# A weighted sum of expert outputs: loads 4 to 10 issued from GpSimd's queue instead of SyncE's

## The chip, the cores and the metric

The kernel runs on one core of a Trainium2 chip. The metric is the device time of one execution, in microseconds (us). The profile comes from one execution recorded by the hardware profiler. DVE is VectorE, ACT is ScalarE, POOL is GpSimd, SP is SyncE and PE is TensorE. "SPq", "ACTq" and "POOLq" are the instruction streams of these engines where they issue transfers.

## The reference

For every token there are two rows of 512 float32 numbers (the outputs of its two experts) and two weights. The result is the weighted sum of the two rows.

```python
batch, seq, hidden, k = 16, 1024, 512, 2
expert_outputs   # (16, 1024, 2, 512) float32, 67.1 MB
combine_weights  # (16, 1024, 2) float32, 0.13 MB
out = np.sum(expert_outputs * combine_weights[..., None], axis=2)   # (16, 1024, 512), 33.6 MB
```

There are 16,384 tokens. For each, 4 KB are read and 2 KB are written, and three arithmetic operations are made for each output number.

## The kernel before

The tokens are dealt out over the 128 partitions of the on-chip memory, 128 to each. The work goes in eleven groups, numbered 0 to 10 by the loop variable `g`. Groups 0 to 9 hold 12 tokens in each partition (6,144 KB to load, 3,072 KB to store), group 10 holds 8 (4,096 KB and 2,048 KB).

Each group has one tile `et` from a pool with four buffers (L50, `bufs=4`). The result of a group is written over the first half of its own tile (`ot`, L66). So a group uses one buffer from its load to the end of its store, and load `g` cannot be issued before store `g-4` has landed. Loads 0 to 3 find free buffers at the start.

For groups 0 to 8, DVE multiplies the whole tile by the weights, which are repeated along 512 columns (L74), and adds the two halves (L75). I call these mult `g` and add `g`. ACT's queue then issues the store (L76). For group 9, ACT scales the first expert's rows (L82, 12 instructions) while DVE scales the second's (L97), and DVE adds them (L98). For group 10, ACT scales one token's row at a time (L82, 8 instructions) and DVE multiplies and adds (L86, 8 instructions). The stores of groups 9 and 10 are issued by SP (L99). The weights come by two small loads from ACT's queue (L58). They are computed on by nothing else.

Who issues what, before: SP issues all eleven loads (L69) and stores 9 and 10. ACT issues the weights and stores 0 to 8. POOL sets four constants at the start and then issues nothing. Each engine works through its own stream in program order, and an instruction that waits holds up all those behind it in that stream. A transfer issued by an engine goes into that engine's transfer queue. The profile calls SP's q1 and ACT's q10. The order of the instructions within each stream is chosen by the framework's scheduler when the kernel is built. It comes from the loop, but is not bound to it.

Before, DVE's stream is mult 0, add 0, mult 1, add 1 and so on to mult 8, add 8, and then L97, L98 and the eight L86. ACT's stream is the two weight loads, stores 0 to 7, eight of group 9's scalings, store 8, the other four scalings, and group 10's eight.

Of the kernel before, what the change touches and what calls it, by code (L numbers as in the profile page):

```python
# [1 line left out]

# [4 lines left out]


@with_exitstack
def kernel(  # L10
    ctx: ExitStack,
    tc: tile.TileContext,
    expert_outputs: bass.AP,
    combine_weights: bass.AP,
    out: bass.AP,
):

    nc = tc.nc  # L20
    b, s, k, h = expert_outputs.shape
    assert k == 2
    n = b * s
    P = nc.NUM_PARTITIONS
    per = n // P
    assert per * P == n
    J, LAST = 12, 8
    main = per - LAST
    assert main % J == 0
    eo = expert_outputs.rearrange("b s k h -> (b s) (k h)")  # L30
    cw = combine_weights.rearrange("b s k -> (b s) k")
    o = out.rearrange("b s h -> (b s) h")

    def rows(x):

        a = x[0 : P * main, :].rearrange("(p t) f -> p t f", p=P)
        b = x[P * main : n, :].rearrange("(p t) f -> p t f", p=P)
        return lambda t, c: a[:, t : t + c, :] if t < main else b[:, t - main : t - main + c, :]

    eo, cw, o = rows(eo), rows(cw), rows(o)  # L40

    dt = mybir.dt.float32
    mult = mybir.AluOpType.mult
    add = mybir.AluOpType.add
    copy = mybir.ActivationFunctionType.Copy

    last = main // J

    wpool = ctx.enter_context(tc.tile_pool(name="w", bufs=1))
    ipool = ctx.enter_context(tc.tile_pool(name="in", bufs=4))  # L50

    wt = wpool.tile([P, per * k], dt)

    warm = wpool.tile([P, 1], dt)
    table = nc.scalar.activation(out=warm, in_=nc.const_aps.tensor(1.0, (P, 1), dt), func=copy)  # L55
    with tc.issue_after(table.ins):
        for t, c in ((0, main), (main, LAST)):
            nc.scalar.dma_start(  # L58
                out=wt[:, k * t : k * (t + c)].rearrange("p (t k) -> p t k", k=k), in_=cw(t, c)
            )  # L60


    for g in range(last + 1):
        et = ipool.tile([P, J, k * h], dt)

        ot = et.rearrange("p j f -> p (j f)")[:, 0 : J * h].rearrange("p (j f) -> p j f", f=h)  # L66
        t0, c = g * J, J if g < last else LAST

        nc.sync.dma_start(out=et[:, 0:c], in_=eo(t0, c))  # L69
        if g < last - 1:  # L70

            wb = wt[:, g * J * k : (g + 1) * J * k].unsqueeze(2).to_broadcast([P, J * k, h])
            ek = et.rearrange("p j (k h) -> p (j k) h", k=k)
            nc.vector.tensor_tensor(out=ek, in0=ek, in1=wb, op=mult)  # L74
            nc.vector.tensor_tensor(out=ot, in0=et[:, :, 0:h], in1=et[:, :, h : 2 * h], op=add)  # L75
            nc.scalar.dma_start(out=o(t0, c), in_=ot)  # L76
            continue


        for i in range(c):  # L80
            t = t0 + i
            nc.scalar.activation(  # L82
                out=et[:, i, 0:h], in_=et[:, i, 0:h], func=copy, scale=wt[:, 2 * t : 2 * t + 1]
            )
            if g == last:
                nc.vector.scalar_tensor_tensor(  # L86
                    out=ot[:, i, :],
                    in0=et[:, i, h : 2 * h],
                    scalar=wt[:, 2 * t + 1 : 2 * t + 2],
                    in1=et[:, i, 0:h],  # L90
                    op0=mult,
                    op1=add,
                )
        if g < last:
            w1 = wt.rearrange("p (t k) -> p t k", k=k)[:, t0 : t0 + c, 1:2]
            x1 = et[:, :, h : 2 * h]
            nc.vector.tensor_tensor(out=x1, in0=x1, in1=w1.to_broadcast([P, c, h]), op=mult)  # L97
            nc.vector.tensor_tensor(out=ot, in0=et[:, :, 0:h], in1=x1, op=add)  # L98
        nc.sync.dma_start(out=o(t0, c), in_=ot[:, 0:c])  # L99


# [1 line left out]
_INS = ['expert_outputs', 'combine_weights']  # L103
_OUTS = [((16, 1024, 512), 'float32')]


# [23 lines left out]
```

## Time and profile before

| what | value |
|---|---|
| time, median of 3 runs | 239.14 us (239.09 to 239.26) |
| the profiled execution: own time | 239.1 us |
| its span in the trace | 237.3 us |
| DVE busy | 194.0 us (82%) |
| ACT busy | 14.0 us (6%) |
| POOL busy | 0.2 us |
| bytes moved | 100.80 MB |
| share of the 16 DMA engines: q1 (SP), q10 (ACT) | 71.0%, 27.9% |
| a mult (L74), an add (L75) | 12.96 us, 6.56 us |
| issue to landing, median: a load of SP, a store of ACT | 29.9 us, 33.0 us |

The profiled execution took 239.1 us, 0.04 below the median of the runs. Its span, from the first instruction to the last, is 237.3 us, so 1.8 us lie around the span. The share of a queue is the time that its packets took, as a share of the whole time of the 16 DMA engines, so the two shares say how nearly the transfers fill the span. "Issue to landing" contains the time that a transfer stands in its queue behind earlier ones, and the time in which it shares the DMA engines with the other queue.

### The profile page before, as it was taken

The numbers are of one execution on the slowest core, as the hardware profiler recorded it, in microseconds if no ns is written. First come the engines' busy times: TensorE is split into PE (matmuls) and PEld (weight loads), VectorE is DVE, ScalarE is ACT, GpSimd is POOL, SyncE is SP. The second block draws the span as 40 slices with busy tenths as digits, with TensorE's granted clock in tenths as the row PEclk, the third lists the DMA queues.
The fourth block names the chain that finished last, engine by engine and source line by source line (L and its number), as shares of the span: only waits on it lengthen the run. The fifth ranks groups of instructions, "written<-read, shape, count | busy, mean of one in ns | idle before, by whom it ended". The sixth has DMA issues, their size and how long they took to land.

```text
span 237.3 us, 153 instructions
## 1 busy us (share of the span) xinstructions
DVE 194.0 (82%) x28; ACT 14.0 (6%) x22; POOL 0.2 (0%) x4
## 2 busy tenths in 40 slices
DVE  0008999999999999999999879969996998785710
ACT  2000000000000000000000000000000000740800
POOL 0000000000000000000000000000000000000000
DMA  7999999989899999999897999999997979999997
GB/s 268 422 524 398 398 415 514 398 356 505 356 439 431 431 464 464 398 398 522 348 522 344 452 431 431 464 464 398 398 522 340 530 340 456 458 403 442 406 434 309
DMA packets 3456, 100.80 MB, mean 425 GB/s; under 512 B 512, under 2 KB 640, under 8 KB 640
## 3 DMA queue, kind: packets, MB, share of 16 engines
q1 hardware_dynamic: 1872, 72.35, 71.0%
q10 hardware_dynamic: 1584, 28.44, 27.9%
HBM read 67.24 MB, written 33.55 MB: 425 GB/s over the span
## 4 chain that ended last, share of the span: by engine, by line
DMA 59%; DVE 33%; ACT 2%; DVEq 0%; ACTq 0%; issue 0%; SPq 0%
DMA out_dram<-et 29%; DMA et<-in_expert_outputs_dram 23%; DVE et L74 22%; DVE et L75 11%; DMA wt<-in_combine_weights_dram 7%; ACT et L82 2%; DVE et L86 1%; DVEq L125 0%; ACTq L125 0%; ACT L55 0%; SPq L69 0%; DVEq L74 0%; ACTq L82 0%
## 5 line engine op out<-in xcount | busy, mean ns | idle before, releaser
L74 DVE TENSOR_TENSOR et<-et,wt 128x12288 f32<-128x12288 f32 x9 | 116.6, 12955 | 25.1 <-DMA wt<-in_combine_weights_dram 18.4
L75 DVE TENSOR_TENSOR et<-et 128x6144 f32<-128x6144 f32 x9 | 59.0, 6557 | 0.3
L82 ACT ACTIVATE et<-et,wt 128x512 f32<-128x512 f32 x20 | 12.5, 707 | 210.2 <-DMA et<-in_expert_outputs_dram 210.2
L86 DVE SCALAR_TENSOR_TENSOR et<-et,wt 128x512 f32<-128x512 f32 x8 | 5.6, 746 | 3.9 <-ACT et L82 3.7
L97 DVE TENSOR_TENSOR et<-et,wt 128x6144 f32<-128x6144 f32 x1 | 6.6, 6558 | 2.2 <-DMA et<-in_expert_outputs_dram 2.2
L98 DVE TENSOR_TENSOR et<-et 128x6144 f32<-128x6144 f32 x1 | 6.6, 6558 | 0.9 <-ACT et L82 0.9
L55 ACT ACT_TABLE_LOAD x1 | 1.3, 1283 | 0.7 <-PEq L114 0.7
L55 ACT ACTIVATE warm<-const-float32-1.0 128x1 f32<-128x1 f32 x1 | 0.2, 204 | 0.0
L114 POOL MEMSET const-bfloat16-1.0<- 128x1 bf16 x1 | 0.1, 103 | 0.0
L114 POOL MEMSET const-uint8-127<- 128x1 uint8 x1 | 0.1, 103 | 0.0
L114 POOL MEMSET const-float32-1.0<- 128x1 f32 x1 | 0.1, 100 | 0.0
L114 POOL MEMSET const-float32-0.0<- 128x1 f32 x1 | 0.1, 99 | 0.2 <-issue 0.2
## 6 DMA issues: line engine op xcount, KB each, us to landing
et<-in_expert_outputs_dram SPq DMA_DIRECT2D x10, 6144.0 KB, 29.9
out_dram<-et ACTq DMA_DIRECT2D x9, 3072.0 KB, 33.0
et<-in_expert_outputs_dram SPq DMA_DIRECT2D x1, 4096.0 KB, 25.1
out_dram<-et SPq DMA_DIRECT2D x1, 3072.0 KB, 14.7
out_dram<-et SPq DMA_DIRECT2D x1, 2048.0 KB, 10.0
wt<-in_combine_weights_dram ACTq DMA_DIRECT2D x1, 120.0 KB, 17.5
wt<-in_combine_weights_dram ACTq DMA_DIRECT2D x1, 8.0 KB, 31.8
```

Of the source, the lines that this page charges most:

```text
L55: table = nc.scalar.activation(out=warm, in_=nc.const_aps.tensor(1.0, (P, 1), dt), func=copy)
L74: nc.vector.tensor_tensor(out=ek, in0=ek, in1=wb, op=mult)
L75: nc.vector.tensor_tensor(out=ot, in0=et[:, :, 0:h], in1=et[:, :, h : 2 * h], op=add)
L82: nc.scalar.activation(out=et[:, i, 0:h], in_=et[:, i, 0:h], func=copy, scale=wt[:, 2 * t : 2 * t + 1])
L86: nc.vector.scalar_tensor_tensor(out=ot[:, i, :], in0=et[:, i, h : 2 * h], scalar=wt[:, 2 * t + 1 : 2 * t + 2], in1=et[:, i, 0:h], op0=mul ...
L97: nc.vector.tensor_tensor(out=x1, in0=x1, in1=w1.to_broadcast([P, c, h]), op=mult)
L98: nc.vector.tensor_tensor(out=ot, in0=et[:, :, 0:h], in1=x1, op=add)
L114: nc = _bacc.Bacc("TRN2", target_bir_lowering=False, num_devices=1)
```

## The change

Loads 0 to 3 are still issued by SP. Loads 4 to 10 are issued by POOL. Nothing else in the source is different but for an empty line that is gone, so all line numbers after it are smaller by one in the profile of the changed kernel.

```diff
-        nc.sync.dma_start(out=et[:, 0:c], in_=eo(t0, c))
+        (nc.sync if g < 4 else nc.gpsimd).dma_start(out=et[:, 0:c], in_=eo(t0, c))
```

What each load waits for is as before: load `g` (4 and up) waits for store `g-4`. The scheduler, however, puts DVE's and ACT's streams in another order when it builds the changed kernel:

```
DVE before: ... mult 3, add 3, mult 4, add 4, mult 5, add 5, mult 6, add 6, mult 7, add 7, mult 8, add 8, L97, L98, ...
DVE after:  ... mult 3, mult 4, add 3, add 4, mult 5, mult 6, add 5, add 6, mult 7, mult 8, add 7, add 8, L96, L97, ...
ACT before: stores 0 to 7, 8 scalings of group 9, store 8, 4 scalings of group 9, 8 of group 10
ACT after:  stores 0 to 6, 11 scalings of group 9, stores 7 and 8, 1 scaling of group 9, 8 of group 10
```

SP's stream after the change is loads 0 to 3, store 9, store 10. POOL's is its four constants and then loads 4 to 10.

## The prediction

> **What bounds the kernel now.** I read the page's totals first, then the slices, then the span cut into stretches, then the chain and the queue's waits, and last the issue times. The page:
>
> ```profile
> span 237.3 us, 153 instructions
> DVE 194.0 (82%) x28; ACT 14.0 (6%) x22; POOL 0.2 (0%) x4
> ...
> DVE  0008999999999999999999879969996998785710
> ...
> DMA  7999999989899999999897999999997979999997
> ...
> q1 hardware_dynamic: 1872, 72.35, 71.0%
> q10 hardware_dynamic: 1584, 28.44, 27.9%
> HBM read 67.24 MB, written 33.55 MB: 425 GB/s over the span
> ```
>
> DVE looks like the busiest engine, but it has holes in the first 18 us and in the last third. The row of DMA has none: the two queues take 98.9% of the DMA engines' span. The same by stretches of about one group (columns: stretch and length, busy time of DVE, ACT and POOL, clock, DMA share, GB/s):
>
> ```profile
> 18.40:38.00 19.60, 19.53 (x3) 0.00 (x0) 0.00 (x0) 1.00 1.02 442
> 38.00:57.40 19.40, 19.36 (x3) 0.00 (x0) 0.00 (x0) 1.00 0.97 405
> ...
> 96.30:115.80 19.50, 19.47 (x3) 0.00 (x0) 0.00 (x0) 1.00 0.99 429
> ...
> 135.40:157.20 21.80, 19.50 (x2) 0.00 (x0) 0.00 (x0) 1.00 1.00 433
> 157.20:181.00 23.80, 19.53 (x3) 0.00 (x0) 0.00 (x0) 1.00 0.99 430
> 181.00:203.00 22.00, 19.60 (x3) 0.09 (x1) 0.00 (x0) 1.00 1.00 430
> ```
>
> The DMA share is 0.97 or more in every stretch from 0.73 us to 220. From 135 us on, DVE has 2 us to spare in every group. It waits for bytes. The chain that ended last and the longest wait of SP's queue say how the bytes are ordered:
>
> ```profile
> 76.94 30.65 DMA out_dram<-et
> 107.59 0.02 SPq L69
> 107.61 0.03 issue
> 107.64 29.93 DMA et<-in_expert_outputs_dram
> ...
> SPq L69 <- DMA out_dram<-et: 189.4, 7, 61.2
> ```
>
> Store 2 lands and load 6 is issued into its buffer, so SP's 189.4 us of waiting are waits for buffers. That wait is not lost time: while load 6 waits to be issued, load 5 is still in SP's queue. The times of issue show the pace:
>
> ```profile
> 64.14 0.33 SPq L69 DMA_DIRECT2D et<-in_expert_outputs_dram  x1
> ...
> 85.93 0.33 SPq L69 DMA_DIRECT2D et<-in_expert_outputs_dram  x1
> ...
> 107.64 0.33 SPq L69 DMA_DIRECT2D et<-in_expert_outputs_dram  x1
> ...
> 226.48 0.34 SPq L99 DMA_DIRECT2D out_dram<-et  x1
> ```
>
> Loads follow one another at 21.75 us, and in that time one load and one store move: 9.437 MB in 21.75 us is 434 GB/s. So the kernel is bound by the DMA engines, which finish whatever stands in the queues. From that rate a load costs 14.5 us of all DMA engines, a store 7.25, load 10 9.67, store 10 4.83 and the weights 0.3. All of it: 10 x 14.5 + 9.67 + 10 x 7.25 + 4.83 + 0.3 = 232.3 us. The last store was issued at 226.48 and took 10.0 to land (the page's issues), so it landed at 236.5. That leaves 4.2 us for the start and all losses on the way. The question about any new order is therefore only: **is there a moment at which all queues are empty?** Each microsecond of such a hole is a microsecond of the result, and nothing else is.
>
> **The change, part by part.**
>
> *Seven issues leave SP, seven come to POOL.* An issue costs SP 0.33 us x 7 = 2.3 us, beside 189.4 us of waiting, so nothing comes free. On SP, stores 9 and 10 stood behind the loads, but went out when L98 and L86 were done, not when SP was free. Their gain is 0. POOL has nothing else after its constants (0.2 us), so nothing is queued behind the new waits there but the next loads, in the order that they had on SP.
>
> *The delay T from the end of a load's wait to its first byte.* No row shows POOL issuing. Lower end: SP's own. The first slice of 5.93 us moved 268 GB/s x 5.93 = 1.59 MB, which is 3.7 us at 434, so bytes flowed from about 2.2 us. The first issue was at 0.73, so T is 1.5 us there. Upper end: POOL is held until the running DVE instruction ends, at most a mult, T = 1.5 + 12.96 = 14.5 us. I take 2.5, near the lower end, because an issue on another engine is the nearest row. What T costs depends on how long the queues last without that load, which I work out below.
>
> *A third queue.* Load 4 is issued at about 64 us, while SP's queue still holds some of load 3. Before, it stood behind load 3, which landed at 72.3 in the trace. Now three queues share. A transfer has 144 packets (1872 of q1 by its 13), 9 for each of 16 DMA engines, and the 128 partitions make 8 of them data: a piece is an eighth, 14.5/8 = 1.81 us for a load and 0.91 for a store. From 64.1 to 72.3 there is room for three pieces of each, so three eighths of load 3 remain, and each now also lets an eighth of load 4 pass: load 3 lands up to 3 x 1.82 = 5.5 later, at 77.7. Mult 3 began at 76.83, so at most 0.9 us of DVE are lost, and load 4 is earlier by as much as load 3 is later. The same bytes move, so cost on the DMA engines is 0. SP's queue is empty after that, and there are two again, POOL's in the place of SP's.
>
> *DVE's new order.* Mult 4 now goes before add 3, so store 3 leaves late. Mult 3 ends at 89.8. Load 4, which landed at 94.0 before (64.14 + 29.9), lands at 92 to 94. Mult 4 then ends at 105 to 107 and add 3 at 111.6 to 113.6. Before, store 3 was issued at 96.40. It is 15 to 17 us late, and load 7 behind it. Meanwhile the queues hold loads 0 to 5 and stores 0 to 2: 6 x 14.5 + 3 x 7.25 + 0.3 = 109.1 us of work, finished between 2.2 + 109.1 = 111.3 and 4.2 + 109.1 = 113.3. What must arrive before that is load 6. Its wait ends when store 2 lands, 107.6 before and up to 1.8 later now (store 1 and 2 also share with load 4). With T = 2.5 it flows at 110.1 to 111.9. So **the first thin place is at about 112 us**, with 0 to 3 us in hand. What is lost there is at most the time until store 3 takes over, about 1.1 us. I take 0.2, as the two intervals hardly overlap.
>
> *The other thin places.* Store 3 and load 6 end at about 134, and load 7 is issued then. Store 4 (add 4 ended 6.6 after add 3, at 118 to 120) waits in ACT's queue and fills 7.25 us: in hand 7.25 - T. Store 4 lands at 147 and releases load 8 with 5 eighths of load 7 to go (9 us in hand). Mult 5 and 6 fill 119 to 145, add 5 ends at 152 and store 5 follows. Store 5 and load 8 end at 178, when store 6 (issued at 158) is in the queue alone: again 7.25 - T for load 9. Store 6 lands at 190, load 10 follows, and load 9 lasts until 200. Load 10 moves alone from 200 to 209.
>
> *ACT's new order.* Store 7 now stands behind eleven scalings that wait for load 9. Add 7 ends at about 197, load 9 lands at 200, and eleven scalings took 6.8 us before, so store 7 leaves by 207 at the latest, and flows at 208.5: before load 10's 9.67 us are over. Cost 0, but with only 1 us in hand. If ACT's queue runs ahead of its scalings (before, store 8 was issued at 203.01, 0.1 us after the first of the eight scalings ahead of it began), there are several. Stores 7 and 8 then fill the time to 224, store 9 (L97 of the changed kernel ends at about 217) to 231, and store 10 (the eight L85 end at 223) to 236. Cost 0. DVE's whole lateness of some 4 us at the last groups lies behind 7 us of queued stores.
>
> *The rate of a load in POOL's queue.* Lower end 0 (same bytes, same pieces). Upper end: the slowest stretch of a group, 38.0 to 57.4, moved 405 GB/s, 7% below 434, and that on 6 x 14.5 + 9.67 = 96.7 us is 6.8 us. I take 0.2, near the lower end, since the stretches at 429 to 442 are the rule.
>
> A rule of the Trainium skill speaks against the change. "SBUF — State Buffer", section "SBUF: two separate sides", says that transfers issued from GpSimd have their descriptors written by GpSimd's cores, and that a DVE instruction in a two-port mode shuts these out until it ends. A mult here takes 12.96 us for 12,288 elements, 1.05 ns each, and has two SBUF inputs. For such instructions the page limits the blocking to GpSimd work that reads SBUF. By that page, writing descriptors would go on, and the sum would stay. If the blocking held, the sum would be that of the first rival. No row of this case shows which.
>
> **Sum.** 237.3 + 0.2 (thin place at 112) + 0.2 (rate) = 237.7 of span, and 1.8 around it: 239.5 us. The profiled execution's 239.1 stands 0.04 below the median, so this is no change by the bound of 0.2% (0.48 us), about what a measurement of this kernel can tell.
>
> **The rivals.**
>
> 1. *POOL is held by DVE (slower).* DVE is busy nearly without a gap from 38 to 200, and each held issue waits for the end of a mult or add. The place that decides is load 7: wait over at 134, when mult 6 has just begun, so issued at 147 and flowing at 148.5 to 149. Store 4 ends at 141. The hole is 7 to 8 us, and a second one of up to 3 can open near 207, at load 10. It decides from a hold of about 5 us on. For it: POOL has not issued anything here beside DVE, so nothing speaks against it in the rows. Against it: POOL's four settings of constants took 0.10 us each, but with DVE idle, so this says little. 237.3 + 7 to 11: 246 to 250 us, and 243 to 246 if only half of a hold is met.
> 2. *The turns are dealt out otherwise.* The pieces of SP and ACT alternate. If POOL's come in larger bundles, a store waits behind most of a load, load 6 is released late and holes of some 2 us open at 112, 158 and 202, up to 5 in all: 241 to 244. If they come in thirds or smaller, stores pass faster, load 4 lands later (98), DVE ends 7 us later and stores 7 and 8 run out before store 9: a hole of 2, 241.
> 3. *Loads from POOL's queue run slower.* Each per cent is 1 us. 1 to 3%: 240.1 to 242.
> 4. *Faster.* It could only come from the 4.2 us that aren't bytes, of which 1.5 + 0.7 are the start. Of the 2.0 left, perhaps 0.5 to 1 goes when loads and stores overlap differently: 238.3 to 238.6. Nothing in the rows points to it.
>
> That the change does nothing is excluded by the streams: POOL has seven loads.
>
> **How the numbers follow.** No hole worth naming: 0.42, with its own range 239.0 to 239.6, and 239.5 in it. Rival 1: 0.16. Rival 2: 0.16. Rival 3: 0.20. Rival 4: 0.06. So faster 0.06, same 0.42, slower 0.52: the cases of slower together outweigh the likeliest single one. Below 239.0 I leave 0.08. Above 244.5 lies some two thirds of rival 1, 0.11. The range is 239.0 to 244.5.
>
> **What would show it.** Right: DMA shares of 0.97 and more in all stretches, loads 7 and 9 flowing before their covering store has ended, SP's wait of 189.4 us gone from its queue and standing in POOL's, store 3 issued at 112 to 114, DVE's last instruction a few us before the last store. Wrong: a stretch at 110 to 113, 134 to 149 or 200 to 210 with a DMA share well under 1 (rivals 1 and 2), or full shares at fewer GB/s (rival 3). The prediction falls if T is above 5 us.

## The result and the profile after

| | before | changed |
|---|---|---|
| median time (5 runs of each, taken in turns) | 239.09 us (238.94 to 239.26) | 241.39 us (241.20 to 242.05) |
| ratio, with its 95% interval | | 1.0094 (1.0071 to 1.0117) |
| the profiled execution: time, span | 239.10, 237.32 us | 241.51, 239.74 us |

The changed kernel is slower by 0.94%, or 2.3 us. The time around the span is the same (1.78 and 1.77 us), so all the difference lies inside the span. The page of the changed kernel:

```profile
span 239.7 us, 156 instructions
DVE 193.2 (81%) x28; ACT 14.0 (6%) x22; POOL 4.0 (2%) x11
...
DVE  0008999999999994999999699999807999999600
...
DMA  7999999999999999999999999999999999999994
...
q0 software_dynamic: 1008, 41.94, 40.8%
q1 hardware_dynamic: 864, 30.41, 29.9%
q10 hardware_dynamic: 1584, 28.44, 27.7%
HBM read 67.24 MB, written 33.55 MB: 420 GB/s over the span
```

POOL's queue is q0. It carries the seven loads (1008 packets are 7 x 144), and q1 keeps six transfers (864). The bytes are the same. The row of DMA still shows no hole, and the three queues take 98.4% of the engines' span. Only the last slice is different: it is at 4 tenths. The same by stretches (columns: stretch and length, busy time of DVE, ACT and POOL, clock, DMA share, GB/s):

```profile
96.30:113.00 16.70, 16.70 (x3) 0.00 (x0) 0.53 (x1) 1.00 1.05 455
113.00:120.00 7.00, 7.00 (x2) 0.00 (x0) 0.00 (x0) 1.00 0.94 407
120.00:135.00 15.00, 12.96 (x2) 0.00 (x0) 0.00 (x0) 1.00 0.96 415
135.00:147.00 12.00, 12.00 (x2) 0.00 (x0) 0.69 (x2) 1.00 1.04 440
...
160.00:181.00 21.00, 12.83 (x1) 0.00 (x0) 0.53 (x1) 1.00 0.98 422
...
203.00:220.00 17.00, 16.90 (x4) 10.09 (x17) 0.00 (x0) 1.00 1.01 428
220.00:235.00 15.00, 5.55 (x9) 1.32 (x3) 0.00 (x0) 1.00 0.99 426
235.00:237.40 2.40, 0.00 (x0) 0.00 (x0) 0.00 (x0) 1.00 0.69 294
237.40:239.70 2.30, 0.00 (x0) 0.00 (x0) 0.00 (x0) 1.00 0.02 7
```

The two ends of the kernel before, in the same view:

```profile
220.00:235.00 15.00, 5.56 (x8) 4.93 (x8) 0.00 (x0) 1.00 1.01 434
235.00:237.30 2.30, 0.00 (x0) 0.00 (x0) 0.00 (x0) 1.00 0.27 114
```

A share a little over or under 1 comes from packets that are counted whole in the stretch in which they start: from 96.30 to 147.00 together the share is 1.01. The thin places of the prediction (112, 134 to 149, 200 to 210) are full. But after 235 us the changed kernel still moves bytes at a share of 0.69, for 2.4 us. Before, the same stretch had 0.27. Then follow 2.3 us with hardly a byte.

What POOL does beside DVE is in the timeline (start, length, engine, line, operation; in brackets the idle time before and what ended it):

```profile
93.26 12.96 DVE L73 TENSOR_TENSOR et<-et,wt 128x12288 f32<-128x12288 f32 x1 [3.30 <-DMA et<-in_expert_outputs_dram]
106.14 13.02 DVE L74 TENSOR_TENSOR et<-et 128x6144 f32<-128x6144 f32 x2
108.23 0.53 POOL L68 DMA_DIRECT2D et<-in_expert_outputs_dram  x1 [17.60 <-issue]
...
134.07 12.96 DVE L73 TENSOR_TENSOR et<-et,wt 128x12288 f32<-128x12288 f32 x1 [2.04 <-DMA et<-in_expert_outputs_dram]
135.50 0.53 POOL L68 DMA_DIRECT2D et<-in_expert_outputs_dram  x1 [26.75 <-issue]
```

Load 7 is issued at 135.50, in the second microsecond of mult 6, and its issue takes 0.53 us. Its first data packet starts at 140.44, while mult 6 runs to 147.03. So POOL is not held until a DVE instruction ends. The waits that stood in SP's queue now stand in POOL's, 189.7 us in all (189.4 before):

```profile
POOL et L68 <- DMA out_dram<-et: 120.6, 4, 64.3
POOL et L68 <- issue: 44.4, 2, 26.8
POOL et L68 <- DVE et L73: 24.7, 1, 24.7
```

**Where the 2.4 us are.** The trace holds, for each transfer, when each of the 16 DMA engines finished its part, and for each packet how long it took. From these I worked out three terms for each kernel. The first is the landing of the last store on the median engine. The second is how far the slowest engine is behind the median one. The third is the time from the slowest engine's landing to the end of the span. The last row is the time that the data packets took, per engine.

| us | before | changed | difference |
|---|---|---|---|
| last store on the median engine | 236.29 | 237.35 | +1.06 |
| slowest engine behind the median | 0.22 | 1.07 | +0.85 |
| end of the span after that | 0.81 | 1.31 | +0.50 |
| sum: the span | 237.32 | 239.73 | +2.41 |
| data packets, per engine | 234.12 | 235.18 | +1.06 |

The median engine is late by just as much as its packets are longer. The rest is unchanged: of the time from the first data packet (1.75 us) to the last landing on the median engine, 0.42 us are not packet time, in both kernels. The packets are the same in number and size, and most take the same time as before (a load's piece 1.815 us, a store's 0.912). Some take up to 0.72 us longer. In the kernel before, such long packets occur in the first microseconds and at about 41 us only, when the first store joins the loads. In the changed kernel they come again at 74 to 82, 139 to 165 and 204 to 207 us.

The engines also get out of step. When load 3 lands at 75.86 us, its parts on ten of the 16 engines are some 2.0 us earlier than on the others, and the first is 2.28 us ahead of the last. Before, they were 0.45 us apart at that load. At store 6 they are 5.6 us apart. The kernel ends with the slowest of them.

The 0.50 us at the end are SP's waits. SP passes a list of semaphores in pairs, 0.06 us for each. In the changed kernel seven more pairs come behind that of the last store (0.45 us). Before, the last store's stood at the end of the list.

### The profile page after: what moved, and what is told of

The parts are those of the page before. It is cut to its first block, busy times and chain, and to the rows that moved or that the text cites. A ratio compares the mean times of both kernels' runs of the same rounds, so it can differ in the third digit from the quotient of the medians.

```text
span 239.7 us, 156 instructions
## 1 busy us (share of the span) xinstructions
DVE 193.2 (81%) x28; ACT 14.0 (6%) x22; POOL 4.0 (2%) x11
## 3 DMA queue, kind: packets, MB, share of 16 engines
q0 software_dynamic: 1008, 41.94, 40.8%
q10 hardware_dynamic: 1584, 28.44, 27.7%
## 4 chain that ended last, share of the span: by engine, by line
DMA 56%; DVE 30%; issue 8%; DVEq 1%; POOLq 0%; ACT 0%
DMA et<-in_expert_outputs_dram 26%; DMA out_dram<-et 22%; DVE et L73 16%; DVE et L74 8%; DMA wt<-in_combine_weights_dram 7%; DVE et L96 3%; DVE et L85 2%; DVE et L97 1%; DVEq L124 0%; POOLq L68 0%; ACT L55 0%; DVEq L85 0%; DVEq L97 0%; DVEq L73 0%
## 5 line engine op out<-in xcount | busy, mean ns | idle before, releaser
L68 POOL DMA_DIRECT2D et<-in_expert_outputs_dram x7 | 3.8, 547 | 189.6 <-DMA out_dram<-et 120.6
```

Source lines behind the costliest of these rows:

```text
L68: (nc.sync if g < 4 else nc.gpsimd).dma_start(out=et[:, 0:c], in_=eo(t0, c))
```

## The experiments

The three terms of all kernels in one table. Times are in microseconds. "Median engine", "slowest" and "end" are the differences against the kernel before, and their sum is that of the spans. "Packets" is the same difference for the data packets per engine. All but the last two columns come from the one profiled execution of each. It was the slowest of its kernel's runs for x3, x5, x6, x8 and x10, and the fastest for x1, x7 and x9. The runs of before that were taken beside these lie within 0.5 us of each other (238.91 to 239.30 beside x1 to x4), but for one of 240.57 beside x5 to x8. So a difference of 0.2 us between two single executions is not read as an effect.

| kernel | profiled | median engine | slowest | end | packets | median time (range) | ratio (95%) |
|---|---|---|---|---|---|---|---|
| before | 239.10 | 0 | 0 | 0 | 0 | 239.09 | 1 |
| changed | 241.51 | +1.06 | +0.85 | +0.50 | +1.06 | 241.39 (241.20 to 242.05) | 1.0094 (1.0071 to 1.0117) |
| x1 queue alone | 239.38 | -0.18 | -0.04 | +0.50 | -0.11 | 239.66 (239.38 to 239.86) | 1.0024 (1.0015 to 1.0033) |
| x2 order alone | 239.57 | +0.11 | +0.37 | 0 | +0.11 | 239.69 (239.55 to 241.20) | 1.0045 (1.0024 to 1.0066) |
| x3 all loads on POOL | 241.32 | +0.72 | +1.25 | +0.26 | +0.33 | 241.07 (240.91 to 241.32) | 1.0086 (1.0072 to 1.0100) |
| x4 loads 9, 10 on POOL | 239.12 | -0.11 | -0.07 | +0.20 | -0.14 | 239.17 (239.11 to 239.44) | 1.0005 (0.9997 to 1.0014) |
| x5 loads 6, 7, 9 | 240.88 | +0.80 | +0.72 | +0.26 | +0.86 | 240.66 (240.61 to 240.88) | 1.0070 (1.0058 to 1.0082) |
| x6 loads 4, 5, 8, 10 | 242.09 | +0.60 | +2.07 | +0.32 | +0.87 | 241.25 (240.78 to 242.09) | 1.0091 (1.0078 to 1.0105) |
| x7 changed, written out | 240.88 | +0.55 | +0.74 | +0.49 | +0.73 | 241.11 (240.88 to 241.27) | 1.0084 (1.0072 to 1.0096) |
| x8 changed, in halves | 240.15 | +0.91 | +0.07 | +0.07 | +1.50 | 240.04 (240.00 to 240.15) | 1.0042 (1.0030 to 1.0054) |
| x9 before, in halves | 240.40 | +0.73 | -0.03 | +0.13 | +1.26 | 240.61 (240.40 to 240.70) | 1.0065 (1.0051 to 1.0078) |
| x10 first pair turned | 241.58 | +1.02 | +0.97 | +0.50 | +1.03 | 241.44 (241.35 to 241.58) | 1.0100 (1.0086 to 1.0113) |
| x11 last pair turned | 239.65 | -0.05 | +0.11 | +0.49 | +0.03 | 239.72 (239.57 to 242.53) | 1.0041 (1.0013 to 1.0068) |
| x12 load 4 after load 3 | 243.50 | +1.47 | +2.44 | +0.50 | +1.65 | 243.28 (241.46 to 243.89) | 1.0149 (1.0117 to 1.0181) |

### The two parts of the change, one at a time: x1 and x2

The change does two things: it gives seven loads to another queue, and it makes the scheduler turn pairs of DVE's instructions round (mult 4 before add 3, and so on) and put ACT's scalings elsewhere. x1 has the new queue and the order of before. That order is fixed by telling the scheduler after which instruction each mult and each scaling is to be issued:

```diff
-            nc.vector.tensor_tensor(out=ek, in0=ek, in1=wb, op=mult)
+            with tc.issue_after(adds[-1].ins) if adds else nullcontext():
+                nc.vector.tensor_tensor(out=ek, in0=ek, in1=wb, op=mult)
...
-            nc.scalar.activation(
...
+            with tc.issue_after(stores[-2 if g < last and i < 8 else -1].ins):
+                scaled = nc.scalar.activation(
```

> Loads 4 to 10 on POOL as in the changed kernel, but DVE's and ACT's streams put back into the order of before. Theory Q (the software queue itself puts the 16 DMA engines out of step and makes some packets longer): about +2 us as in the changed kernel, 240.6 to 241.6, with the 16 landings of the last store spread over 1.5 us or more (0.40 before, 2.06 in the changed kernel). Theory O (the new order of DVE and ACT makes it, by late stores): back to 239.1 within 0.5, spread 0.4.

x2 has all loads on SP and the new order written out:

```diff
-        (nc.sync if g < 4 else nc.gpsimd).dma_start(out=et[:, 0:c], in_=eo(t0, c))
+        nc.sync.dma_start(out=et[:, 0:c], in_=eo(t0, c))
...
+            late.append((et, ot, t0))
+            if g in (3, 5, 7):
+                continue
+            for e1, o1, t1 in late:
+                with tc.issue_after(mul.ins):
+                    adds.append(
...
```

> All loads on SP as before, but DVE's and ACT's streams in the order of the changed kernel. Theory Q: 239.1 within 0.5, landings of the last store within 0.5 us of each other. Theory O: 240.6 to 241.6 and a spread over 1.5 us.

The queue alone gives 239.66, or +0.57 us by the medians, and the order alone 239.69, or +0.60. Both together give +2.30, which is 1.1 us more than the sum of the two medians. But x2's runs differ: four of the six lie at 239.55 to 239.69, the other two at 240.45 and 241.20. By the ratios the parts add up to 0.69% and the whole is 0.94%, with intervals of 0.09 to 0.23 on each, so what the two give beyond their sum is not clear of noise. Both theories wanted more than 240.6 us from one of the two kernels and a time within 0.5 us of before from the other, and neither got it. In x1 the whole difference of the profiled execution is the end (+0.50): the bytes land a little earlier than before. The queue with the order of before keeps the engines in step all the way (load 3 lands at 75.65 us with 0.32 us between the first engine and the last) and has no long packets that before has not. In x2 the engines are out of step from 133 us on, but less, and its packets are only 0.11 us longer. So in the executions that were profiled neither part has the loss in it, and the changed kernel has. All ten runs of the changed kernel and of its repetition x7 (below) took 240.88 us or more, and all eleven of x1 239.86 or less. The two longer runs of x2 left no trace, so it isn't known what they lost.

### How many loads on POOL: x3 and x4

Both keep the order of before. x3 gives POOL all loads, x4 the last two:

```diff
-        (nc.sync if g < 4 else nc.gpsimd).dma_start(out=et[:, 0:c], in_=eo(t0, c))
+        nc.gpsimd.dma_start(out=et[:, 0:c], in_=eo(t0, c))
```

```diff
-        (nc.sync if g < 4 else nc.gpsimd).dma_start(out=et[:, 0:c], in_=eo(t0, c))
+        (nc.sync if g < 9 else nc.gpsimd).dma_start(out=et[:, 0:c], in_=eo(t0, c))
```

> All eleven loads on POOL, order of before. There is then no time in which SP's and POOL's queues hold loads together. Theory Q with a cost per load of POOL: 7 loads cost 2.3 us, so 11 cost 3 to 4, 242 to 243. Theory M (the mixing of three queues around load 3 and load 4 puts the engines out of step, and they stay so): within 0.5 us of before, spread of the last store's landings about 0.5.

> Only loads 9 and 10 on POOL, order of before. Theory Q with a cost per load: 2 of 7 loads, about +0.7 us, 239.6 to 240.0. Theory M: there is again a time with loads in both queues (load 8 on SP, load 9 on POOL), so the spread of the landings appears there too, 1.5 us or more, and the time is 240.0 to 241.

The page of x3:

```profile
span 239.5 us, 157 instructions
...
q0 software_dynamic: 1584, 67.11, 65.4%
```

All eleven loads are in q0 there (1584 packets are 11 x 144). The time is 241.07, but the terms are other ones than in the changed kernel. The first data packet starts at 2.68 us, against 1.75 with SP. The engines are 2.6 us apart from load 2 on, and the slowest ends 1.47 us behind the median. Yet there are no long packets after 60 us. So engines can be out of step, and cost time at the end, without long packets. x4 can't be told from before (1.0005, 0.9997 to 1.0014). Its engines too were 2.2 us apart at 184 to 198 us, but they were in step again at the end. The loss is therefore no price per load. Theory Q's price per load (242 to 243 for x3, 239.6 to 240.0 for x4) and theory M (within 0.5 us of before for x3, 240 to 241 for x4) both missed both times.

### Which loads: x5 and x6

Both have the new order. In x5 POOL issues the loads that flow when SP's or POOL's queue has run dry of loads (6, 7 and 9), in x6 it issues the others of the seven:

```diff
-        (nc.sync if g < 4 else nc.gpsimd).dma_start(out=et[:, 0:c], in_=eo(t0, c))
+        (nc.gpsimd if g in (6, 7, 9) else nc.sync).dma_start(out=et[:, 0:c], in_=eo(t0, c))
```

```diff
-        (nc.sync if g < 4 else nc.gpsimd).dma_start(out=et[:, 0:c], in_=eo(t0, c))
+        (nc.gpsimd if g in (4, 5, 8, 10) else nc.sync).dma_start(out=et[:, 0:c], in_=eo(t0, c))
```

> Streams of DVE and ACT as in the changed kernel. Only loads 6, 7 and 9 are issued by POOL: those that in the changed kernel come when the queues are about to run empty (at 108, 135 and 180 us). Theory T (the DMA engines fall out of step where a load of POOL meets nearly empty queues): most of the changed kernel's loss, 240.7 to 241.5, spread of the last store's landings over 1.3 us. Theory N (each load of POOL costs about the same): 3 of 7 loads on top of what the order alone costs (239.7), about 240.4.

> The complement: POOL issues loads 4, 5, 8 and 10, which find other transfers in the queues, and SP the rest. Streams of DVE and ACT as in the changed kernel. Theory T: little above the order alone (239.7) and the POOL queue's end (0.3), 239.7 to 240.2. Theory N: 4 of 7 loads, about 240.7.

Theory T gave 239.7 to 240.2 for x6 and theory N 240.7. Measured are 241.25, so T is missed by more than 1 us, and N by 0.5. x5 gives 240.66. Theory T's 240.7 to 241.5 for x5 is just missed, and theory N's 240.4 by 0.3. Each half of the loads carries most of the loss by itself, and the halves add up to more than the whole. In both kernels nearly all the added packet time falls at 200 to 210 us, where load 10 flows and stores 7 and 8 join it: 12.8 and 11.8 us, summed over 16 engines. The changed kernel has 3.6 us there, and x2, with the same order and all loads on SP, 0.6. So neither theory stands: the loads that start in an emptying queue are not the cause, and their number is not either.

### The changed kernel again: x7

The order of the changed kernel is written out here as in x2, with the queues of the changed kernel. It says whether what was seen in one trace comes again.

> The changed kernel's queues and streams, with its order of DVE and ACT written out instead of found by the scheduler. All theories: 241.2 to 242.1 as the changed kernel. Its profile tells whether the engines fall out of step at the same place again (load 3 at 75.9 us had its 16 landings 2.28 apart): the same place speaks for a cause in the schedule, another place for chance.

It does: 241.11 us, a little under the 241.2 to 242.1 that were expected. Load 3 lands at 75.82, and its parts are 2.27 us apart again, with eleven engines early. There are long packets at 80 to 90, 130 to 160 and 200 to 210 us. Single engines differ from one execution to the next, the places do not.

### Smaller pieces: x8 and x9

If the loss comes of long pieces of load and store that meet on an engine, shorter pieces should lessen it. Each load and each store is issued as two transfers of half the tokens, in the changed kernel (x8) and in the one before (x9):

```diff
-        (nc.sync if g < 4 else nc.gpsimd).dma_start(out=et[:, 0:c], in_=eo(t0, c))
+        for u in (0, c // 2):
+            (nc.sync if g < 4 else nc.gpsimd).dma_start(out=et[:, u : u + c // 2], in_=eo(t0 + u, c // 2))
```

```diff
-        nc.sync.dma_start(out=et[:, 0:c], in_=eo(t0, c))
+        for u in (0, c // 2):
+            nc.sync.dma_start(out=et[:, u : u + c // 2], in_=eo(t0 + u, c // 2))
...
-            nc.scalar.dma_start(out=o(t0, c), in_=ot)
+            for u in (0, 6):
+                stores.append(nc.scalar.dma_start(out=o(t0 + u, 6), in_=ot[:, u : u + 6]))
```

> The changed kernel's queues and streams, with each load and store cut into two transfers of half the tokens, so that a piece on a DMA engine lasts half as long (0.91 and 0.46 us). Theory P (the engines are out of step by turns of whole pieces, and the end waits for the slowest): spread of the last landings about half of 2.06, and the loss against before about half, 240.1 to 240.6. If the loss has nothing to do with the length of a piece: 241.2 or more, as there are twice as many issues.

> The kernel before (all loads on SP, its own order) with each load and store cut into two transfers of half the tokens. It is the control for the changed kernel in halves (240.04). Theory P (the loss comes by turns of whole pieces, so halves take most of it away): cutting costs something by itself, because the packets of that kernel added up to 1.7 us more per DMA engine; so 239.6 to 240.0, and changed minus before in halves 0.1 to 0.5. If the loss has nothing to do with the length of a piece: 237.8 to 238.2, so that the difference of 2 us stays.

The page of x8, and then that of x9:

```profile
span 238.4 us, 199 instructions
...
q0 software_dynamic: 2016, 41.94, 40.9%
```

```profile
span 238.1 us, 190 instructions
...
q1 hardware_dynamic: 3744, 72.35, 71.1%
```

The packets of q0 have doubled (1008 to 2016), the bytes have not changed. The spans of the two are 0.2 us apart, where those of the whole transfers are 2.4 apart. All five runs of each agree: spans of 238.2 to 238.4 us in x8 and 238.1 to 238.4 in x9. (By the medians x8 is 0.57 us below x9. Of that, 0.46 lie around the span: 2.25 us in x9's profiled execution, 1.79 in x8's.) The slowest engine of x8 ends 0.29 us behind the median, not 1.07. Halving costs something in itself: the data packets of x9 take 1.26 us more per engine than before. Those of x8 take 0.24 us more than those of x9, where whole transfers had 1.06 between them. So with halved transfers the changed kernel's own loss is gone from the span, as theory P has it. The times that theory P gave were missed (x8 240.04 for 240.1 to 240.6, x9 240.61 for 239.6 to 240.0). Halving also doubles the number of transfers, so these runs don't show that it is the length of a piece that counts. The kernel before, with whole transfers, remains faster than both.

### Which turned pair: x10 and x11

Both have POOL's queue for loads 4 to 10. In x10 only the first pair is turned (mult 4 before add 3), in x11 only the last (mult 8 before add 7), with the place of ACT's scalings that goes with it in the changed kernel:

```diff
-            nc.vector.tensor_tensor(out=ek, in0=ek, in1=wb, op=mult)
-            nc.vector.tensor_tensor(out=ot, in0=et[:, :, 0:h], in1=et[:, :, h : 2 * h], op=add)
...
+            late.append((et, ot, t0))
+            if g == 3:
+                continue
...
```

```diff
...
+            late.append((et, ot, t0))
+            if g == 7:
+                continue
...
```

> Loads 4 to 10 on POOL. Of the three pairs of groups whose adds come after both mults in the changed kernel only the first (3 and 4) is left so; the rest of DVE's and ACT's streams is as before. Theory F (what counts is that the engines fall out of step once, early; they stay so to the end): close to the full loss, 240.7 to 241.4, and a spread over 1.3 at the end. Theory S (each stretch with loads only or stores only costs its own part): a third of what lies between 239.7 and 241.4, about 240.2.

> As the run before, but only the last pair (7 and 8) is left as in the changed kernel, with ACT's two stores behind the eleven scalings. Theory F: the engines are in step until 180 us and have little time to drift apart, 239.7 to 240.2. Theory S: a third, about 240.2, or more if the stretch of loads only at 195 to 205 us is the dear one (long packets there were 0.25 us per engine of the changed kernel's 1.06).

x10 has the whole loss (241.44), x11 none in its landings (239.72, and in its profiled execution +0.49 of +0.55 are the end). One of x11's eight runs took 242.53 us, though, and left no trace. Three stretches of x1, where no pair is turned:

```profile
160.00:181.00 21.00, 19.52 (x2) 0.00 (x0) 0.53 (x1) 1.00 1.00 431
...
220.00:235.00 15.00, 5.57 (x8) 5.01 (x8) 0.00 (x0) 1.00 0.98 423
235.00:240.00 5.00, 0.00 (x0) 0.00 (x0) 0.00 (x0) 1.00 0.12 49
```

and the same of x10:

```profile
160.00:181.00 21.00, 16.55 (x2) 0.00 (x0) 0.53 (x1) 1.00 0.98 422
...
220.00:235.00 15.00, 8.02 (x9) 5.01 (x8) 0.00 (x0) 1.00 0.97 416
235.00:240.00 5.00, 0.00 (x0) 0.00 (x0) 0.00 (x0) 1.00 0.38 161
```

The stretches stay full (0.97 to 1.00), but a few GB/s are missing, and what was not moved is moved after 235 us: 161 GB/s x 5 us is 0.81 MB, against 0.25 in x1. Those 0.56 MB are 1.3 us at the prediction's 434 GB/s. Turning the pair delays store 3, so that loads flow nearly alone until 113 us, and a store flows alone later: load 7's first data packet starts at 140.66 here, and in the changed kernel no data packet of a load starts between 130.96 and 140.44. Load 3 lands 2.35 us apart on the 16 engines here, at 75.86, as in the changed kernel. The long packets come at 82 to 103 and above all at 139 to 154 us (12.2 us at 130 to 160, summed over 16 engines). x11's engines are out of step as well, by up to 2.39 us from 76 to 195 us, but its packets keep their length and the engines are back in step at the end. So being out of step does not by itself make packets long. Theory F came near with both times (240.7 to 241.4 and 239.7 to 240.2), but by luck: its reason was that x11's engines would be in step until 180 us, and they fell out of step as early as x10's.

### Without the meeting of load 3 and load 4: x12

In the changed kernel, x7 and x10, load 3 (SP) and load 4 (POOL) flow beside each other at 65 to 76 us, and then the engines are out of step. x12 is the changed kernel with load 4 made to wait for load 3's landing:

```diff
+        if g == 4:
+            dep = mybir.DependencyInfo(mybir.DependencyClass.Sync, mybir.DependencyReason.DATA)
+            tc.add_manual_dep(loads[4].ins, loads[3].ins.name, dep, reason="after load 3")
```

> The changed kernel's queues and streams, with one more wait: POOL issues load 4 only when load 3 has landed, so that SP's and POOL's queues never hold loads together. Load 4 then flows from about 75 us, while store 1 still has 2 to 3 us of work. Theory X (both are needed for the whole loss: the engines out of step from the time with loads in both queues, and the new order's stretches of loads only and stores only): in step at load 3 (landings within 0.6 us at 72 us), and near the order alone plus the longer end, 239.9 to 240.5. If the mixing at load 3 and 4 is not a cause: 241.0 to 241.5 as the changed kernel.

Measured are 243.28 us (four of the six runs at 243.13 to 243.89, two at 241.46), not theory X's 239.9 to 240.5. The timeline shows that load 4 is issued after load 3 has landed:

```profile
72.75 0.66 POOL L69 DMA_DIRECT2D et<-in_expert_outputs_dram  x1 [72.30 <-DMA et<-in_expert_outputs_dram]
...
77.53 0.53 POOL L69 DMA_DIRECT2D et<-in_expert_outputs_dram  x1 [4.12 <-DMA out_dram<-et]
```

and so do the stretches:

```profile
72.00:76.00 4.00, 4.00 (x1) 0.00 (x0) 0.66 (x1) 1.00 1.00 430
76.00:85.00 9.00, 9.00 (x2) 0.00 (x0) 0.53 (x1) 1.00 1.02 415
85.00:96.30 11.30, 4.74 (x1) 0.00 (x0) 0.00 (x0) 1.00 0.98 418
```

Load 3 lands at 72.10 in step (0.33 us apart), and store 1 follows at 76.95 in step too. Load 4's first data packet starts at 75.96. From there on packets are long all the same: 10.4 us at 70 to 90 and 10.3 at 200 to 210, summed over 16 engines. The DMA share stays at 0.98 to 1.02 with 415 to 418 GB/s: full engines, fewer bytes. The engines are 1.7 us apart when load 4 lands at 98.42, and 3.0 at the end. So the meeting of the two loads puts engines out of step, but the loss doesn't need it. What the meeting costs in the changed kernel isn't shown, because the edit makes a new stretch of stores only (72 to 76 us), and the first long packets follow it. By the median this is the slowest kernel here.

**What is shown and what is open.** Shown: no hole opened, and the changed kernel's loss consists of long packets, engines out of step, and 0.5 us at the end. With loads 4 to 10 in POOL's queue the turned order brings this loss in all ten runs (the changed kernel and x7), the first turned pair is enough for it (x10), and without a turned pair it is not there (x1). In halved transfers the first two parts are nearly the same with and without the change. Not shown: that the loss needs POOL's queue. On SP the turned order took 239.55 to 239.69 us in four runs of x2 and 240.45 and 241.20 in two, so POOL's queue may only make a loss regular that the order can have by itself. All loads on POOL (x3) cost as much without any turned pair, but by engines out of step rather than by long packets. Open: why a packet takes longer at these places. Many of the long packets of x5, x6, x10 and x12 come where loads and stores join again after a stretch in which one kind flowed alone, in a kernel in which loads have flowed through POOL's queue. But not every such place has them: x11 has one at 205 us, with the same queues and the same order of ACT, and x5 one at 140 us, after ten microseconds in which no load packet starts, and neither has long packets there. I don't know what tells them apart. No version here beats the kernel before.

## Why the prediction was right and where it was wrong

The forecast was 239.5 us, the range 239.0 to 244.5, and slower had the larger chance. Measured are 241.39. The range held, the likeliest case (239.0 to 239.6) did not. That the range held is in part luck: its upper part was made for holes behind POOL's issues, for turns dealt otherwise and for a slower queue, and the loss came by none of these as they were meant.

**The bound: right, but stated too narrowly.** The DMA engines are the bound and no hole opened: shares of 0.94 to 1.05 in all stretches up to 235 us, and the same time without a packet. (The sign asked for 0.97 and more. The two stretches at 0.94 and 0.96 lie between two at 1.05 and 1.04, and the four together have 1.01.) But "each microsecond of such a hole is a microsecond of the result, and nothing else is" is wrong. There were no holes, and 2.4 us were lost. Three things were missing from it: packets can become longer, so that a full engine moves fewer bytes; the end is that of the slowest of 16 engines, not that of an average one; and SP's waits after the last landing.

**The streams: right.** The times that were worked out, against those of the changed kernel:

| | predicted | measured |
|---|---|---|
| load 3 lands | up to 77.7 | 75.86 |
| load 4 lands | 92 to 94 | 93.24 |
| store 3 issued | 111.6 to 113.6 | 112.72 |
| load 7 issued | 134 | 135.50 |
| load 8 issued (store 4 landed) | 147 | 146.84 |
| load 9 issued | 178 | 180.37 |
| load 10 issued | 190 | 193.39 |

Loads 9 and 10 are 2.4 and 3.4 us late. The long packets explain this in part at most: x2, whose packets are only 0.11 us longer per engine than before, issues them at 178.54 and 193.08, so for load 10 the working itself was 3 us early. SP's wait of 189.4 us for buffers is gone from SP, as expected. DVE ended at 225.8, over 10 us before the last store landed, so its lateness cost nothing. ACT's new order cost no hole either.

**T: too small, and over its bound.** The prediction took 2.5 us from the end of a load's wait to its first byte, and was to fall above 5. Load 7's wait ended when store 3 landed at 134.97, and its first data packet starts at 140.44: 5.47 us. For load 9 it is 5.26 (179.80 to 185.06). So this sign of being wrong came true. Of it, some 0.55 us pass before POOL issues (SP issued 0.05 to 0.09 after a landing before), and 4.94 and 4.69 from the issue to the first data packet. This contains the turns of the store that is flowing: SP's loads take 3.64 and 3.92 from their issue at the same two places in x2. With nothing else flowing, POOL needs 1.44 (load 0 of x3) and SP 1.02. So from the issue on, POOL's own share is 0.4 to 1.3 us more than SP's. No hole came of it, because store 4 and store 6 had 7.25 us to cover it. Whether the longer stretch of stores only has a part in the long packets behind it is open. The term of 0.2 us for the thin place at 112 was 0.

**The rate of a load in POOL's queue: this term failed.** It was put at 0.2 us, with 0 and 6.8 for its ends. The packets were longer by 1.06 us per engine. As the term was meant, a property of the queue, even 0.2 is too much: x1 has the same queue and its packets are 0.11 us shorter than before. The lengthening came with the turned order in that queue, and the sum had no term for that. The stretch that was used for the upper end (38.0 to 57.4 at 405 GB/s) does contain the event, the long packets when the first store joins. It was read as a slow stretch, not as a loss that happens where streams join and can happen again.

**Two terms that the sum did not have.** The slowest engine (+0.85) and SP's waits at the end (+0.50). The sum took the time from the last landing to the end as it was.

**The rivals.** Rival 1 (POOL held by DVE) fell: the issue of load 7 during mult 6, and its data 6.6 us before that mult ended. Rival 2 (turns dealt otherwise) had 241 to 244, which fits the time but not the mechanism: it wanted holes, and there are none. Rival 3 (a slower rate, full shares at fewer GB/s) had 240.1 to 242, and its sign in the profile is the one that came: 420 GB/s over the span at 98.4%, against 425 at 98.9%. It is the nearest one, and explains 1.06 of the 2.41 us. Rival 4 (faster) fell: the changed kernel is slower, and the 0.2 us by which x1's bytes landed earlier than before is no more than single executions differ by.

**The rule that was weighed.** "SBUF — State Buffer", section "SBUF: two separate sides", of the Trainium skill limits the blocking of such DVE instructions to GpSimd work that reads SBUF. The trace agrees that these ones, mult and add in float32 with two SBUF inputs, do not shut POOL out (load 7, 135.50 and 140.44 inside 134.07 to 147.03). Another rule bears on the result. "DMA: Bandwidth & Descriptors", section "Issuing engines are not separate DMA queues", says that issuing from several engines saves only the time that the issue takes on a sequencer. The runs agree that there is nothing to win: 0.33 us of SP's time per load became 0.53 to 0.66 of POOL's. They go further: it cost 0.57 us by itself, and 2.30 with the order that came with it.

## What to carry to other kernels

In a kernel that is bound by the DMA engines, a new queue or a new order is not judged by holes alone: look at how long packets of one size take along the span, how far apart the 16 engines land, and what the program still waits for after the last landing. When a load's issuing engine is changed, look first at what the scheduler does with the other engines' streams, and test the queue and the order apart: by the medians each alone cost 0.6 us here, and both together 2.3. Look at every run and not at the median alone, since x2, x11 and x12 have runs 0.8 to 2.8 us away from the rest. Where two versions differ by a change of overlap, run both with halved transfers: here the difference of their spans went from 2.4 to 0.2 us.

## What the runs showed of the hardware that was not expected

- In every kernel here with whole transfers, load packets lengthen from 1.815 us to 2.2 to 2.4 (medians of the kernels) when the first store joins them at about 41 us. In the kernel before this costs 8.4 us summed over 16 engines, or 0.5 us per engine.
- The parts of one transfer on the 16 engines can be 5.6 us apart (store 6 of the changed kernel) or 6.8 (store 4 of x12); they can come into step again (x4, x11).
- POOL's issue of a load takes 0.53 to 0.66 us, SP's 0.33. It starts 0.53 to 0.65 us after the landing that it waited for, SP's 0.05 to 0.09.
- Transfers of half the size cost 1.26 us more packet time per engine over the whole kernel (x9), with the same bytes.
- SP's waits for the semaphores at the end of the program take 0.06 us for each pair, and how many pairs stand behind that of the last store is worth 0.5 us.
